# Two-layer hybrid trunk: the order of the first mixer, its startup and weight reuse, the place of an output product, and casts moved to ScalarE

## The chip, the cores and the metric

The kernel runs on one NeuronCore of a Trainium2 chip. The metric is device time in microseconds (us) of one execution, the median of three runs, of which one was recorded by the hardware profiler with the instructions, waits and transfers of every engine.

## The reference

The input is a sequence of 1024 tokens with 1024 features in float32, and one conditioning vector c. Two layers follow each other, each with a token mixer and an FFN. Every sub-layer is normalised and modulated (adaLN): six vectors per layer come out of a product of c with a large matrix, and give a scale, a shift and a gate.

```
    cond = jax.nn.silu(c)
    for i in range(DEPTH):
        mod = (cond @ ada_w[i] + ada_b[i])[:, None, :]
        sh1, sc1, g1, sh2, sc2, g2 = jnp.split(mod, N_MOD, axis=-1)
        ...
        h = rmsnorm(x, norm_mix_g[i]) * (1.0 + sc1) + sh1
        ...
        x = x + g1 * y
        h = rmsnorm(x, norm_ffn_g[i]) * (1.0 + sc2) + sh2
        x = x + g2 * (jnp.square(jax.nn.relu(h @ ffn_w1[i])) @ ffn_w2[i])
```

Here y is the output of the token mixer for h. The first mixer (RG-LRU, width 1280) is a product to two branches, a causal convolution of width 4 on one, a GELU on the other, two sigmoid gates out of 256 x 256 blocks, then the recurrence h[t] = a[t] h[t-1] + sqrt(1 - a[t]^2) (i[t] x[t]), a product with the gate branch and a product back to 1024. The second mixer (DSA) has 16 query heads of 64 on one shared key and value; an indexer of 8 heads scores all earlier tokens, the 256 best of a token take part in its softmax. The FFN is 1024 to 4096 to 1024 with squared ReLU.

## The kernel before, in words

Activations lie transposed, features on the 128 partitions and tokens along the row; the 1024 tokens go as two halves of 512 (h = 0 and 1). Every float32 product is made of three passes in a 32-bit reduced format, `mm3` (L337 to L339): a value is split into a high part (a cast, `wh`) and a low part (the remainder, `wl`), and high x high, low activation x high weight and high activation x low weight are added in PSUM. Weights pass through `weights()`: a block of 512 KB is loaded raw by SP's queue, ScalarE casts `wh` (L322), POOL subtracts for `wl` (L325). The first time a block is used, both parts are written to a DRAM copy (`part`, L330), and the second half reads these two parts back instead.

The program is written as Python generators and a few lists: what stands in the text order is the order on each engine. `pump` and `mix` put pieces of background lists (`fill`, `bg`) between the main steps. The adaLN work of later sub-layers is a series of `mac` steps in `fill` (a transfer of 256 KB on ScalarE's queue, then L433 or L435 on VectorE), ended by `fin` (transposes, L442).

**Startup** (`startup`, 0 to about 90 us) computes the scale and shift of the first norm for 8 blocks of 128 features: for each block VectorE sums eight 128 x 256 blocks of the matrix (`mac`, L519 and L521), TensorE transposes the sums (`cols`, L527), and VectorE reduces. Between them go the first six output blocks of the mixer's input product for the first half; then x's second half is loaded, squared and transposed (`turn_x`, L469), and its norm taken.

**The first mixer** (`mixer0`) has 5 groups (u) of 256 channels and runs a list `plan` of steps, each named by a letter, groups and the half: c (input product and convolution), g (GELU branch), l (gates and recurrence, `lru`), o (output product of the groups named). `lru` has two tiles, each with tanh, exp, tanh, square on ScalarE, and then two square roots (L652), which need another table of functions than the tanh and exp do; the table is loaded by an instruction of its own, ACT_TABLE_LOAD. In the end ScalarE casts the result (L663), POOL subtracts (L664), and output matmuls need both. The residual sum of the output products is L682. A norm is three parts: `stat` (squares summed by one-column matmuls, L71), `bc` (a broadcast to all partitions, L84), and `apply` (L98 to L104).

**FFN and layer 1.** `f1` is the first FFN product, with squared ReLU, `f2` the second, added to the residual by VectorE (L174). In layer 1, `kv_steps`, `qi_steps` and `q_group` make the keys, index queries and queries per token block and head group; `split_heads` makes the two parts of the queries (a VectorE cast L818, a POOL subtraction L819), and `turn4` transposes them (L827). `idx_steps` and `topk_steps` score the tokens and find the threshold. `attention(h)` goes through 16 units (token block, head group g, parity): scores (L1071, L1072), mask (L1083), exponential (L1089), reciprocal (L1092), POOL's normalising (L1094), transposes (L1099), product with the values (L1111, L1112). `proj_out(h, g1, g)` is the output product of head group g. In the last stage `store` transposes the result back (L1193) and writes it.

## Time and profile before

| | before |
|---|---|
| median of three runs | 2618.0 us (2617.76 to 2620.06) |
| profiled execution: time | 2617.35 us |
| profiled execution: span | 2615.6 us |
| TensorE busy | 2427.1 us (93%) |
| VectorE busy | 1546.9 us (59%) |
| ScalarE busy | 1231.0 us (47%) |
| POOL busy | 996.4 us (38%) |

The time of the profiled execution lies 1.75 us above its span. The busy time of TensorE contains matmuls at the lower of the clock's two levels; the mean granted clock over the span is 0.97. The profile's engine names are PE (TensorE), DVE (VectorE), ACT (ScalarE), POOL and SP.

### The profile page before, as it was taken

The numbers are of one execution on the slowest core, as the hardware profiler recorded it, in microseconds if no ns is written. First come the engines' busy times: TensorE is split into PE (matmuls) and PEld (weight loads), VectorE is DVE, ScalarE is ACT, GpSimd is POOL, SyncE is SP. The second block draws the span as 40 slices with busy tenths as digits, with TensorE's granted clock in tenths as the row PEclk, the third lists the DMA queues.
The fourth block names the chain that finished last, engine by engine and source line by source line (L and its number), as shares of the span: only waits on it lengthen the run. The fifth ranks groups of instructions, "written<-read, shape, count | busy, mean of one in ns | idle before, by whom it ended". The sixth has DMA issues, their size and how long they took to land. (4 is left out here: it accounts for less than half of the span.)

```text
span 2615.6 us, 30703 instructions
## 1 busy us (share of the span) xinstructions
PE 2427.1 (93%) x10834; PEld 1948.6 (74%) x10834; DVE 1546.9 (59%) x2873; ACT 1231.0 (47%) x2158; POOL 996.4 (38%) x584
## 2 busy tenths in 40 slices
PE   5689899898999999999996998999998998999999
PEld 3567678676788888888776876888887786788887
DVE  8677775579934421376686875575579894421212
ACT  3466463541122143235535767768753884433322
POOL 3454411222121244230136932223235996444342
PEclk7899999999999999999998998999999999999999
DMA  8677656326611278754431212223240003322231
GB/s 241 243 251 248 211 208 238 123 81 216 202 49 49 97 250 292 276 174 163 145 99 27 96 51 73 84 82 101 82 137 9 1 9 121 113 89 97 89 102 60
DMA packets 202748, 345.14 MB, mean 132 GB/s; under 512 B 19594, under 2 KB 109410, under 8 KB 202594
## 3 DMA queue, kind: packets, MB, share of 16 engines
q1 hardware_dynamic: 173648, 297.91, 33.6%
q10 hardware_dynamic: 28946, 45.27, 5.2%
q8 instruction: 85, 1.39, 0.2%
q14 instruction: 69, 0.57, 0.1%
HBM read 270.77 MB, written 72.35 MB: 131 GB/s over the span
## 5 line engine op out<-in xcount | busy, mean ns | idle before, releaser
L325 POOL TENSOR_TENSOR wl<-raw,wh 128x1024 fp32r<-128x1024 f32 (+2 forms) x242 | 597.1, 2476 | 1175.1 <-ACT wh L322 1128.2
L322 ACT CAST wh<-raw 128x1024 fp32r<-128x1024 f32 (+2 forms) x275 | 282.7, 1031 | 594.6 <-PE ps L338 270.7
L337 PE MATMUL ps<-a,wh 128*128 128x512 f32 x1152 | 462.5, 404 | 41.1 <-DVE a L682 13.9
L338 PE MATMUL ps<-a,wh 128*128 128x512 f32 x1152 | 461.4, 401 | 3.7 <-POOL a L664 2.2
L339 PE MATMUL ps<-a,wl 128*128 128x512 f32 x1152 | 459.4, 399 | 0.0
L337 PE MATMUL pd<-a,wh 128*128 128x512 f32 x1072 | 429.1, 401 | 21.6 <-DVE xc L595 13.8
L338 PE MATMUL pd<-a,wh 128*128 128x512 f32 x1072 | 428.0, 399 | 7.1 <-DVE a L100 5.7
L339 PE MATMUL pd<-a,wl 128*128 128x512 f32 x1072 | 427.2, 399 | 0.0
L174 DVE SCALAR_TENSOR_TENSOR a<-ps,mod,a 128x512 f32<-128x512 f32 x352 | 260.1, 745 | 264.2 <-PE ps L339 263.5
L337 PEld LDWEIGHTS ps<-a,wh 128*128 128x128 f32 x1152 | 220.0, 191 | 100.8 <-DVE a L682 16.0
L338 PEld LDWEIGHTS ps<-a,wh 128*128 128x128 f32 x1152 | 219.7, 191 | 57.9 <-POOL a L664 4.0
L339 PEld LDWEIGHTS ps<-a,wl 128*128 128x128 f32 x1152 | 219.2, 190 | 53.5
L337 PEld LDWEIGHTS pd<-a,wh 128*128 128x128 f32 x1072 | 202.4, 189 | 74.0 <-issue 14.5
L338 PEld LDWEIGHTS pd<-a,wh 128*128 128x128 f32 x1072 | 203.1, 189 | 59.8 <-DVE a L100 8.2
L339 PEld LDWEIGHTS pd<-a,wl 128*128 128x128 f32 x1072 | 203.1, 189 | 49.1
L1094 POOL TENSOR_SCALAR s<-s,rr 128x128 f32<-128x128 f32 (+7 forms) x128 | 224.9, 1789 | 22.3 <-DVE rr L1092 22.3
L337 PE MATMUL ps<-hid,wh 128*128 128x512 f32 x512 | 204.6, 400 | 12.9 <-DVE a L174 12.9
L978 ACT ACTIVATE signs<-sc,tc 128x384 int8<-128x384 f32 (+5 forms) x186 | 164.1, 882 | 92.9 <-DVE tc L993 79.4
L339 PE MATMUL ps<-hid,wl 128*128 128x512 f32 x512 | 204.0, 398 | 0.0
L338 PE MATMUL ps<-hid,wh 128*128 128x512 f32 x512 | 204.0, 398 | 0.0
L435 DVE SCALAR_TENSOR_TENSOR a<-a,cond,a 128x512 f32<-128x512 f32 x140 | 132.0, 974 | 45.0 <-DMA a<-in_ada_w_dram 44.3
L337 PEld LDWEIGHTS ps<-hid,wh 128*128 128x128 f32 x512 | 97.2, 190 | 39.4 <-DVE a L174 15.2
(270 smaller groups left out, 3715.9 us busy)
## 6 DMA issues: line engine op xcount, KB each, us to landing
raw<-in_ffn_w_dram SPq DMA_DIRECT2D x192, 512.0 KB, 3.6
a<-in_ada_w_dram ACTq DMA_DIRECT2D x160, 256.0 KB, 3.7
part<-wh SPq DMA_DIRECT2D x61, 512.0 KB, 3.6
part<-wl SPq DMA_DIRECT2D x61, 512.0 KB, 3.0
wh<-part SPq DMA_DIRECT2D x61, 512.0 KB, 3.3
wl<-part SPq DMA_DIRECT2D x61, 512.0 KB, 4.5
raw<-in_a_w_in_dram SPq DMA_DIRECT2D x20, 512.0 KB, 6.4
st<-in_ada_w_dram SPq DMA_DIRECT2D x32, 256.0 KB, 4.2
```

The costliest lines, as they stand in the source:

```text
L174: nc.vector.scalar_tensor_tensor(xt, ps, self.g2[:, m:m + 1], xt, op0=OP.mult, op1=OP.add)
L322: nc.scalar.copy(wh, raw)
L325: eng.tensor_tensor(wl, raw, wh.bitcast(FT), op=OP.subtract)
L337: pe.matmul(out, wh, xh, start=start, stop=False)
L338: pe.matmul(out, wh, xl, start=False, stop=False)
L339: pe.matmul(out, wl, xh, start=False, stop=stop)
L435: nc.vector.scalar_tensor_tensor(a, r, s, a, op0=OP.mult, op1=OP.add)
L978: A.activation(self.signs[:, 0:L], sc, AF.Sign, bias=0.0 if neg is None else neg.bitcast(FT), accum_out=n)
L1094: G.tensor_scalar(sl[e][:, 0:L], sl[e][:, 0:L], r[:, e:e + 1], None, op0=OP.mult)
```

## The change

The change has eight parts.

1. **Startup columns.** For the blocks 0 to 3 (NS = 4) the adaLN sums are made by TensorE: for scale and shift, eight one-column matmuls each (L559 of the changed kernel). For the blocks 4 to 7 only the scale is, and VectorE sums 128 x 128 for the shift. x's second half, its squares, transposes and norm sums become a step `second` at the head of the mixer's plan.
2. **The plan of the first mixer** is another list: each recurrence comes one step after its convolution with another projection or an output product between, the output products are "o010", "o20", "o340" and "o011", "o21", "o341", the adaLN `fin`, the norms and the FFN's first block take other places, and one `pump` follows each step.
3. **One square root** in `lru` covers both tiles (128 x 1024).
4. **Weights.** Mixer blocks keep only `wl` in DRAM; at the second use the raw block is loaded again, ScalarE casts it again, and `wl` is read back. FFN blocks are kept as before. Output weights of attention are now kept in this way too. The writes of the copies are issued two blocks later.
5. **adaLN loads** are issued one `mac` ahead.
6. **FFN of layer 0:** the first four steps of `f2` for half 0 come ahead of the first product of half 1.
7. **Layer 1's queries:** in query groups ScalarE does the first cast of `split_heads`. The transposes of group g = 1 go to a list of their own, which the attention takes up after its first unit. The indexer steps of blocks 6 and 7 (11 of 16) go between and after `stat` and `bc` of the FFN's norm, no longer into the FFN's background. Before the last attention, two steps of `f2` go between the two query groups.
8. **The output product** of head group 0 for the last attention runs in that attention's background from unit 12 on. `store` goes in pieces: the first half's between `stat` and `bc` of the last norm, a part of the second half's into the last FFN.

```
+            while (k, 0) not in st:
+                self.loads.pop(0)()
+            if self.loads:
+                self.loads.pop(0)()
...
         def cols(kt):
             ps = self.ps()
-            for e in range(2):
-                nc.tensor.transpose(ps[:, e * P:(e + 1) * P], sums[kt][:, e * P:(e + 1) * P], self.ident)
-            t = self.small([P, 2], "mt")
-            V.tensor_reduce(t, ps[:, 0:256].rearrange("p (e k) -> p e k", e=2), axis=AX.X, op=OP.add)
+            for e in range(2 if kt < NS else 1):
+                for k in range(KT):
+                    nc.tensor.matmul(ps[:, e:e + 1], view(kt, k, e), self.cond[:, k:k + 1],
+                                     start=k == 0, stop=k == KT - 1)
...
-            for m in range(2):
-                A.activation(v[m], v[m], AF.Sqrt, scale=0.25)
+            A.activation(vv, vv, AF.Sqrt, scale=0.25)
...
+        if kept:
+            nc.sync.dma_start(wl.bitcast(FT), kept[0])
+            return wh, wl
...
-            for w in (wh, wl):
+            for w in (wl,) if isinstance(key[0], str) else (wh, wl):
                 d = self.dram.tile([P] + shape, FT, name=self.nm("part"))
-                nc.sync.dma_start(d, w.bitcast(FT))
+                self.late.append((d, w.bitcast(FT)))
...
-            plan = ["g10", "l00", "l10", "c20", "g20", "o010", "l20",
-                    "c30", "g30", "l30", nB, "c40", "g40", "o230", "l40",
-                    "c01", "g01", "o40", "l01", "c11", "g11", "l11", "c21", "g21", "o011", "l21",
-                    lambda: N["f0", 0].stat(), "c31", "g31", "c41", "l31", "g41", "o231", "l41", nA,
-                    lambda: f1(0), "o41", f1b]
+            plan = [lambda: self.second(), "g10", "l00", "c20", "l10", "g20", "c30", fin, "o010", "l20", "g30", "c40",
+                    "l30", "g40", nB, "o20", "l40", "c01", "g01", "o340", "l01", "c11", stat0, "g11", "c21", "l11",
+                    "g21", "c31", "o011", "l21", "g31", "c41", "l31", "g41", nA, "o21", "l41", f1a, "o341", f1b]
...
-            nc.vector.tensor_copy(zv[:, :, 0:64], rv)
+            (nc.scalar.copy if parity else nc.vector.tensor_copy)(zv[:, :, 0:64], rv)
...
+            if k and self.late_turns:
+                late()
             self.pump()
...
+            some(4)
             N["f1", 0].stat()
+            some(4)
             N["f1", 0].bc()
             hf[0] = N["f1", 0].apply(mod[1, 4], mod[1, 3])
-            for t in (6, 7):
-                self.fill += self.idx_steps(t) + [lambda t=t: self.fill.extend(self.topk_steps(t))]
+            some(3)
+            self.fill += heads + self.topk_steps(6) + self.topk_steps(7)
...
+            def background():
+                yield from f2
+                while self.units < 12:
+                    yield
+                self.reload(1)
+                self.rate = 0.45
+                yield from self.proj_out(1, mod[1, 2], 0)
+
+            self.bg, self.rate = background(), 0.8
             self.banks(False)
             self.attention(1, before)
             self.finish()
-            self.reload(1)
-            run(self.proj_out(1, mod[1, 2], 0))
             run(self.proj_out(1, mod[1, 2], 1, sqs("f1")))
```

On TensorE, in the startup, before (`ma` is VectorE's sum, `pd` and `ps` are PSUM tiles):

```order
L469 MATMUL ps_178<-ident,st_97 128x128
L84 MATMUL ps_195<-nl_189,ones 128x512
L527 MATMUL ps_291<-ident,ma_282 128x128 x2
L527 MATMUL ps_329<-ident,ma_311 128x128 x2
L337 MATMUL pd_198<-a_301,wh_307 128x512
```

And now, at the same place (`cond` is c, `st` the loaded block of the matrix):

```order
L492 MATMUL ps_178<-ident,st_97 128x128
L84 MATMUL ps_195<-nl_189,ones 128x512
L559 MATMUL ps_284<-cond,st_204 128x1 x4
L559 MATMUL ps_284<-cond,st_207 128x1 x4
L559 MATMUL ps_323<-cond,st_214 128x1 x4
L559 MATMUL ps_323<-cond,st_217 128x1 x4
L351 MATMUL pd_200<-a_304,wh_310 128x512
```

The two transposes of each of VectorE's sums have become one-column matmuls straight on the loaded blocks (each of the rows shown for a block stands twice, for scale and shift), so that nothing on VectorE is between the load and TensorE's sums.

On TensorE, at the last recurrence of the first mixer, before (`ps_3882` is a gate product of that recurrence, L84 the broadcast of the norm behind it, `ps_4044` the output product that needs the recurrence):

```order
L338 MATMUL ps_3882<-a_3559,wh_3843 128x512
L339 MATMUL ps_3882<-a_3558,wl_3845 128x512
L84 MATMUL ps_3915<-nl_3324,ones 128x512
L337 MATMUL ps_4044<-a_3903,wh_4040 128x512
L338 MATMUL ps_4044<-a_3904,wh_4040 128x512
L339 MATMUL ps_4044<-a_3903,wl_4042 128x512
```

And now (`ps_3898` is the gate product, `pd_3942` the FFN's first block, `ps_4011` the output product):

```order
L352 MATMUL ps_3898<-a_3568,wh_3860 128x512
L353 MATMUL ps_3898<-a_3567,wl_3861 128x512
L353 MATMUL pd_3942<-a_3750,wl_3939 128x512
L351 MATMUL pd_3942<-a_3756,wh_3938 128x512
L352 MATMUL pd_3942<-a_3757,wh_3938 128x512
L353 MATMUL pd_3942<-a_3756,wl_3939 128x512
...
L351 MATMUL ps_4011<-a_3634,wh_4007 128x512
```

The FFN's first block stands between the last gate products and the output product (13 matmuls of it behind the gates), and the norm's broadcast has moved ahead of all of it.

On TensorE, at the beginning of the first attention, before (`a` of L1071 are keys, L827 are query transposes, L1099 the softmax's first transposes, L778 a key and value product):

```order
L1071 MATMUL ps_11055<-a_8195,a_10235 128x384
L1072 MATMUL ps_11055<-a_8197,a_10235 128x384
L827 MATMUL ps_11097<-identR,a_10782 128x128 x4
L827 MATMUL ps_11103<-identR,a_10785 128x128 x4
...
L827 MATMUL ps_11127<-identR,a_10813 128x128 x4
L1099 MATMUL ps_11133<-ident,s_10857 128x128 x4
L778 MATMUL ps_11142<-wh_10887,a_10609 128x328
```

And now (L1124, L874, L1152 and L825 to L827 are the same operations in the changed kernel):

```order
L1124 MATMUL ps_11084<-a_8224,a_10264 128x384
L1125 MATMUL ps_11084<-a_8226,a_10264 128x384
L1152 MATMUL ps_11126<-ident,s_10886 128x128 x4
L825 MATMUL ps_11135<-wh_10916,a_10638 128x328
L826 MATMUL ps_11135<-wl_10917,a_10638 128x328
...
L1152 MATMUL ps_11139<-ident,s_10969 128x128 x4
...
L874 MATMUL ps_11151<-identR,a_10811 128x128 x4
```

The six groups of query transposes that stood ahead of the softmax's first transposes are now behind them and spread over the key and value products.

## Rows read from the trace of the kernel before

**Rows 1.** Page: engine, busy us (share of the span), instructions.

```profile
PE 2427.1 (93%) x10834; PEld 1948.6 (74%) x10834; DVE 1546.9 (59%) x2873; ACT 1231.0 (47%) x2158; POOL 996.4 (38%) x584
```

**Rows 2.** Stages: length; busy PE, PEld, DVE, ACT, POOL (records); PEclk, DMA share, GB/s.

```profile
0.00:84.00 84.00, 48.78 (x189) 35.22 (x189) 66.34 (x148) 31.47 (x45) 33.37 (x25) 0.84 0.75 227
84.00:155.00 71.00, 50.10 (x205) 39.16 (x205) 44.72 (x57) 43.09 (x67) 30.56 (x16) 0.86 0.72 249
155.00:260.00 105.00, 98.13 (x408) 76.41 (x408) 81.89 (x93) 62.66 (x87) 55.72 (x25) 0.98 0.74 257
260.00:336.00 76.00, 56.93 (x222) 44.02 (x221) 56.66 (x73) 36.94 (x48) 31.62 (x15) 0.89 0.64 214
336.00:510.00 174.00, 170.78 (x740) 136.45 (x738) 107.18 (x154) 89.16 (x124) 28.99 (x20) 1.00 0.56 200
510.00:570.00 60.00, 50.48 (x201) 38.49 (x202) 47.59 (x64) 29.20 (x43) 14.02 (x7) 0.89 0.12 39
570.00:705.00 135.00, 120.56 (x511) 94.60 (x510) 120.26 (x162) 25.99 (x36) 29.09 (x11) 0.96 0.65 209
...
1330.00:1475.00 145.00, 119.75 (x632) 103.61 (x631) 108.50 (x297) 82.71 (x223) 94.66 (x95) 0.86 0.18 54
...
1540.00:1600.00 60.00, 47.78 (x206) 38.12 (x205) 47.89 (x93) 37.05 (x77) 9.02 (x6) 0.86 0.14 44
1600.00:1980.00 380.00, 380.00 (x1636) 306.09 (x1635) 232.50 (x524) 257.59 (x436) 110.46 (x48) 1.00 0.29 93
1980.00:2250.00 270.00, 243.94 (x1288) 196.47 (x1287) 204.25 (x416) 170.66 (x332) 211.12 (x125) 0.96 0.13 42
...
2600.00:2615.60 15.60, 9.91 (x59) 8.22 (x57) 4.83 (x7) 2.25 (x4) 0.00 (x0) 0.93 0.36 135
```

**Rows 3.** The instructions of line L521: min/median/max ns, first and last start.

```profile
L521 DVE SCALAR_TENSOR_TENSOR ma<-st,cond,ma x56: 470/478/2147, 17.0 to 73.0; 128x256 f32<-128x256 f32 x56
```

**Rows 4.** Timeline, startup and mixer: start, length, engine, instruction [idle before, releaser].

```profile
28.33 0.66 PE L527 MATMUL ps<-ident,ma 128*128 128x128 f32 x2 [9.91 <-DVE ma L521]
...
97.11 2.25 DVE L433 TENSOR_SCALAR a<-a,cond 128x512 f32<-128x512 f32 x1 [2.18 <-DMA a<-in_ada_w_dram]
...
103.86 0.77 PE L337 MATMUL pd<-a,wh 128*128 128x512 f32 x1 [11.44 <-DVE xc L595]
...
265.93 0.79 PE L337 MATMUL ps<-a,wh 128*128 128x512 f32 x1 [5.59 <-DVE ns L102]
...
332.82 0.79 PE L337 MATMUL ps<-a,wh 128*128 128x512 f32 x1 [7.67 <-DVE a L682]
...
509.49 0.63 ACT L652 ACTIVATE v<-v 128x512 f32<-128x512 f32 x1
510.14 1.28 ACT L645 ACT_TABLE_LOAD   x1
...
516.20 0.80 PE L337 MATMUL ps<-a,wh 128*128 128x512 f32 x1 [9.08 <-ACT a L663]
```

**Rows 5.** Timeline of TensorE, layer 1, columns as in rows 4.

```profile
1395.11 0.75 PE L827 MATMUL ps<-identR,a 128*128 128x128 f32 x4 [7.28 <-POOL a L819]
...
1575.08 1.87 PE L71 MATMUL ps<-ones,nl 128*128 128x1 f32 x8 [6.18 <-DVE nl L63]
1581.40 2.05 PE L84 MATMUL ps<-nl,ones 128*128 128x512 f32 x2 [4.45 <-DVE tl L991]
...
2178.47 0.47 PE L1099 MATMUL ps<-ident,s 128*128 128x128 f32 x1 [4.33 <-POOL s L1094]
...
2236.83 1.05 PE L71 MATMUL ps<-ones,nl 128*128 128x1 f32 x8 [2.69 <-DVE nl L63]
```

**Rows 6.** A stretch of the startup, columns as in rows 2.

```profile
19.00:40.00 21.00, 7.96 (x19) 5.38 (x20) 20.90 (x41) 6.42 (x10) 11.14 (x8) 0.51 1.03 276
```

**Rows 7.** Page: ScalarE's weight casts, xcount | busy, mean ns | idle before, releaser.

```profile
L322 ACT CAST wh<-raw 128x1024 fp32r<-128x1024 f32 (+2 forms) x275 | 282.7, 1031 | 594.6 <-PE ps L338 270.7
```

More of the change, by code (lines that the diff above doesn't have):

```diff
@@ L421, in ada, with load @@
         st = {}
+        def load(k):
+            for c in range(2):
+                st[k, c] = self.tile()
+                o = j * D + c * 512
+                nc.scalar.dma_start(st[k, c], self.i["ada_w"][l, k * P:(k + 1) * P, o:o + 512])
+        self.loads += [lambda k=k: load(k) for k in range(KT)]
         def mac(k):
@@ L927, in turn @@
                 self.turned.add((T, g, p))
[L929 removed]
+            turns.append([lambda p=p, turn=turn: turn(p) for p in range(2)])
             yield
@@ L1049, in attention, with late @@
         heads = [(u, i) for u in units for i in range(0, 4, step)]
+        def late():
+            for f in self.late_turns.pop(0):
+                f()
         def qk(u, i0):
@@ L1297, in run @@
             self.ada_fill([(1, 1, self.gmix(1)), (1, 0), (1, 2), (1, 4, self.gffn(1)), (1, 3), (1, 5)])
-            F.load2(0, 0), F.load2(0, 1)
+            F.load2(0, 0)
+            f2 = F.f2_steps([0], 0)
+            for _ in range(4):
+                next(f2)
             F.f1(0, 1), F.f1(1, 1)
+            F.load2(0, 1)
+            run(f2)
+            F.f2([0], 1)
             for p in range(NJ):
```

170 lines of the change are left out of this document (106 added, 64 removed).

## The prediction

> **What bounds the kernel now.** I read the page's table of engines first, then one table of engine busy time by stage, and then, in the stages with loss, the timeline rows of TensorE's waits. The table of engines [rows 1] shows TensorE busy for 93% of the span, so only work that TensorE does at the lower clock, its waits, or work taken off it can pay. The table by stage [rows 2] says where these are. In the saturated attention and FFN stretch of 1600 to 1980 TensorE has 380.00 us of work in 380.00 us at full clock, and one record takes 380/1636 = 0.232 us; nothing can be won there. The losses lie in the other rows: idle time is the stage's length less TensorE's busy time, and a stage with a mean granted clock c spent 2(1-c) of its length at the lower level (1.2 GHz). Idle are: 0 to 84: 35 us; 84 to 155: 21; 155 to 260: 7; 260 to 336: 19; 336 to 510: 3; 510 to 570: 10; 570 to 705: 14; 1330 to 1475: 25; 1540 to 1600: 12; 1980 to 2250: 26; 2600 to the end: 6. Together that is 178 us, plus what the lower clock costs behind each wait. The change rearranges the order in nearly all of these stages and hardly touches the saturated ones, so I go stage by stage, with the profiled execution (2617.35 us, 0.65 us under the median) as base.
>
> **Startup, 0 to 84.** Here the adaLN column sums run on VectorE: the instruction of L521 takes 0.478 us at the median, and TensorE waits 9.91 us for one at 28.33 [rows 3, 4]. VectorE is busy 66 of these 84 us [rows 2]. The change takes the row blocks 0 to 3 off it altogether (4 x 8 x 0.478 = 15.3 us) and halves the other four in width (between 0 and 7.6 us). In return TensorE gets 96 one-column matmuls in the program, which are 192 records. Their form is not in the startup before; the nearest rows are the eight one-column records of L71, once 1.05 us and once 1.87 us [rows 5], so 0.131 or 0.234 us each, and 25 or 45 us for all. TensorE's 144 wide records of the stage need 144 x 0.232 = 33 us; most of the other 45, transposes, lie before that wait. The wait at 28.33 begins at 28.33 - 9.91 = 18.4 us; columns and wide records from there on, without a wait, end at 18 + 25 + 33 = 76 against 84, a gain of 8, of which I take 4 since not every wait goes. But in 19 to 40 the granted clock is 0.51 [rows 6]. If it stays there while blocks 0 to 3 are summed, their 128 records cost 128 x 0.234 = 30 us and the 72 wide ones of these blocks 72 x 0.464 = 33; the other 64 one-column records (8) and the other 72 wide ones (17) follow: 18 + 30 + 33 + 8 + 17 = 106, 22 us late. The term is a gain of 4, its bounds a gain of 14 (the later waits of the stage shortened too) and a loss of 22.
>
> **84 to 155.** TensorE waits 11.44 us at 103.86 for the first convolution, VectorE having stood at 97.11 for an adaLN weight transfer with that convolution queued behind it [rows 4]. After the change these transfers are issued one step ahead, and the transposes of x's second half go behind the first convolutions. The gap and its lower clock cost about 11 + 6; the transposes and squares that have moved come back later (some 32 short records and four copies, about 5). I take 10 of the 21 idle us, between 3 and 18.
>
> **155 to 570, the mixer.** The plan now puts a projection between a convolution and its recurrence. In 155 to 260 only 7 us are idle, I take 4. In 260 to 336 two waits stand, 5.59 us at 265.93 and 7.67 at 332.82 [rows 4], 13.3 together, both behind one long VectorE series with nothing else for TensorE to do; the new order has an FFN norm and projections elsewhere, and I take 12 of the 19 us (bounds 4 and 22, with the clock). In 510 to 570 the wait of 9.08 us for the last recurrence's cast [rows 4] is what the order rows show filled by FFN matmuls; VectorE has 48 of 60 us there, so some wait remains, and I take 6 (bounds 0 and 15).
>
> The square root of both tiles in one instruction halves the table loads, from 41 in the program to 21. One lasts 1.28 us [rows 4], so ScalarE does 20 x 1.28 = 26 us less. It is off TensorE's path except at the last recurrence, where one load and one cast stand between the data and the wait; that is inside the 6. The Trainium skill ("ScalarE: Activation LUTs", section "What ACT_TABLE_LOAD costs") counts a drain of about 1.38 us beside each load, 2.66 us in all; by it the saving on ScalarE would be an estimated 53 us, and the last wait 1.4 us more to win. The rows here show no such drain, for the square root ends at 509.49 + 0.63 = 510.12 and the next load begins at 510.14 [rows 4].
>
> The price of this is in the weights: for the mixer's second use of a block only the low part is read back, and the high part is cast again on ScalarE. That is 29 more casts of 1.031 us [rows 7], 30 us, in 260 to 570. Between 336 and 510 ScalarE is busy 89 of 174 us [rows 2], so the casts fit beside TensorE's work; I count -2, with bounds of 0 and 30. In layer 1 eight casts and eight subtractions on POOL fall away in the last stage, off the path.
>
> **570 to 705.** VectorE is busy 120 of 135 us there [rows 2]: the FFN's second product is written back by it. The first four steps of the second product now come before the first product of the other half, so that its write-back begins earlier and is spread over more of TensorE's work. I take 5 of 14 us, with bounds 0 and 10.
>
> **Layer 1.** At 1395.11 TensorE waits 7.28 us for POOL's splitting of the query, ahead of the first attention work [rows 5], and the granted clock of the stage is 0.86, so some 41 us pass at the lower level. The order rows show these query transposes behind the first transposes of the softmax now, and half of the split's first casts go to ScalarE, which has 83 of 145 us [rows 2]. To be had are these 7.28 us and about 10 of clock, half of the 20 that 41 us at the lower level can cost; I take 9 (0 to 17). In 1540 to 1600 the norm's waits of 6.18 and 4.45 us [rows 5] get eleven indexer steps around them: I take 7 (0 to 14), since the clock is held too. In 1980 to 2250 the second part of the queries gets two FFN steps in between (3 of the idle us), and the output product of the first heads goes into the last attention's background. POOL is busy 211 of 270 us there and TensorE waits on its normalising, 4.33 us at 2178.47 [rows 5]. POOL's work does not shrink, so the attention itself cannot end much sooner: only TensorE's idle time in it can be filled, not all 26 us; I take 8 more (0 to 14). The last stage: stores of one half drawn forward, 2 of its 6 idle us.
>
> **The sum.** 4 + 10 + 4 + 12 - 2 + 6 + 5 + 9 + 7 + 3 + 8 + 2 = 68 us. From 2617 that is 2549, and against the median 2550.
>
> **Rivals.**
> A. *The startup stays at the lower clock.* For it: 0.51 in 19 to 40, in which TensorE has work for 8 of 21 us [rows 6], and single-column work is small. Against it: these columns give TensorE something to do in the very gap. The startup ends 22 late instead of 4 early: 2550 + 26 = 2576. The Trainium skill ("TensorE: Matmul & The Clock Gate", section "HAM oscillation — how this bites in real kernels") says that groups of matmuls with waits between them start cold each time; by that rule this rival happens, and the stretch at 0.51 agrees with it.
> B. *Layer 1's engines, not its order, are the limit.* POOL is full in the last attention and VectorE has 48 of 60 us in 1540 to 1600 [rows 2]. Then 9 + 7 + 8 fall away: 2574.
> C. *The repeated casts are late, and the kernel gets slower.* The place is the mixer's second half, 260 to 570. A cast there stands in ScalarE's order behind a table load (1.28), two exponentials or roots and their waits, so a weight may come 3.2 us late (1.28 and three instructions of about 0.6), and 29 x 3.2 = 93 us more: 2550 + 93 = 2643. It decides from 68/29 = 2.3 us for each on. Against it: three raw buffers, and ScalarE idle half the time [rows 2].
> D. *VectorE carries the mixer.* It is busy 45 of 71, 82 of 105, 57 of 76 and 48 of 60 us in the stages from 84 on [rows 2], and a new order leaves that work as it is. The waits only move, and 10 + 4 + 12 + 6 go: 2582.
>
> **How the numbers follow.** A measurement of this kernel tells about 0.2% (5 us) from no change. The forecast, 2530 to 2566 by the stage bounds, gets 0.62; A 0.13 (2576), B 0.10 (2574), D 0.09 (2582), C 0.06 (2643). All but C lie more than 0.2% below 2618; I leave 0.02 for several of A, B and D together ending within 0.2%, taken from them. So faster 0.92, same 0.02, slower 0.06. The range from 2520 to 2586 holds the forecast, A, B and D one at a time, and leaves out C, most mixtures and a part of the bounds on the gain's side.
>
> **What would show it.** Right: the one-column rows in the startup at 0.13 us and the last block's matmuls done before 80; no TensorE gap over 5 us behind a recurrence; TensorE's gaps at about 1395 and 1575 gone, and the stages' mean clock near 1. TensorE's busy time would fall only by the cold stretches. Wrong: casts of L328 as the releaser of TensorE's waits (C); the startup's clock at 0.5 past 50 us (A); VectorE as the releaser of gaps as long as now in the mixer (D); POOL still ahead of gaps over 4 us with the output product left behind (B).

## The result, and the profile after

The changed kernel takes 2588.93 us (median of four runs, 2585.56 to 2592.21), the kernel before in the same measurement 2617.88 us: the ratio is 0.9884, 95% interval 0.9872 to 0.9897. It is faster by 29 us. The forecast was 2550 us with a range of 2520 to 2586: the sign is right, the gain is less than half of the 68 us, and the time lies 3 us above the range. The profiled execution has a span of 2587.3 us.

TensorE's row of the page, which answers to [rows 1]:

```profile
PE 2449.9 (95%) x11014; PEld 1976.0 (76%) x11014; DVE 1500.7 (58%) x2802; ACT 1234.9 (48%) x2187; POOL 965.9 (37%) x575
```

TensorE is busy 23 us more in a span 28 us shorter, with 180 records more: its idle time has fallen, and a good part of the place has been filled with the new columns. Where it still waits is seen by stage; the stretches are cut at the same events as in the table below (columns as in [rows 2]), and the second and the fourth are shorter ones around two waits:

```profile
0.00:92.60 92.60, 77.62 (x369) 66.39 (x370) 42.91 (x106) 31.37 (x44) 33.22 (x26) 0.83 0.64 196
85.00:108.00 23.00, 7.91 (x37) 5.81 (x37) 13.92 (x17) 8.96 (x14) 11.12 (x5) 0.83 1.01 356
108.00:170.00 62.00, 60.87 (x261) 48.81 (x262) 43.70 (x53) 42.52 (x73) 31.66 (x16) 0.95 0.46 156
170.00:185.20 15.20, 1.09 (x6) 0.59 (x5) 12.08 (x16) 8.42 (x12) 7.32 (x4) 0.68 0.73 235
185.20:312.00 126.80, 116.25 (x481) 92.28 (x481) 106.75 (x125) 64.81 (x89) 59.12 (x27) 0.94 0.55 180
312.00:554.00 242.00, 230.33 (x966) 181.46 (x967) 155.95 (x222) 132.71 (x180) 48.64 (x31) 0.97 0.51 171
1343.00:1512.00 169.00, 149.01 (x844) 127.48 (x845) 132.63 (x355) 118.41 (x314) 124.98 (x131) 0.94 0.32 109
1991.00:2209.00 218.00, 204.84 (x1138) 165.22 (x1137) 164.01 (x337) 155.78 (x310) 175.50 (x103) 0.99 0.19 65
```

The times at which the same events stand in the two traces (us from the start of the span) tell where the 28 us come from:

| event | before | after | gained so far |
|---|---|---|---|
| first convolution of the mixer (ScalarE) | 92.53 | 92.62 | -0.1 |
| first convolution of the second half | 308.39 | 302.28 | 6.1 |
| last recurrence's cast of the mixer | 520.43 | 521.32 | -0.9 |
| first matmul of the FFN's second product | 557.95 | 553.95 | 4.0 |
| norm ahead of layer 1 (first half) | 1103.52 | 1095.17 | 8.4 |
| norm of the other half | 1353.40 | 1342.90 | 10.5 |
| first attention, last product with values | 1532.35 | 1512.42 | 19.9 |
| last attention, first scores | 2012.42 | 1991.18 | 21.2 |
| last norm's `stat` | 2236.83 | 2208.64 | 28.2 |
| end of the last engine instruction (a copy on VectorE) | 2611.89 | 2583.56 | 28.3 |

Startup and mixer together gave 4 us, where the forecast had 34 (4 + 10 + 4 + 12 - 2 + 6). Layer 0's FFN gave 4, the first attention 9, what lies between it and the last norm 8. Three rows of the table say less than they seem to. In the nine kernels of this document that share this startup, the changed one and eight of the experiments, the first convolution stands between 87.2 and 93.5 us, so a difference of 5 us there is no result. Ahead of the first convolution of the second half the old list has one group's output product more ("o230" for "o20"), so the 6.1 us are in part moved work. And two steps of the FFN's second product now stand ahead of the last attention's first scores and not behind them. The columns and TensorE's main waits, in the timeline of the kernel after (they answer to [rows 4, 5]):

```profile
18.80 10.95 PE L559 MATMUL ps<-cond,st 128*128 128x1 f32 x64
...
107.80 0.76 PE L351 MATMUL pd<-a,wh 128*128 128x512 f32 x1 [12.30 <-DVE xc L641]
...
185.12 1.94 PE L465 MATMUL ps<-ident,a 128*128 128x128 f32 x8 [14.11 <-DVE a L458]
...
268.87 0.79 PE L351 MATMUL ps<-a,wh 128*128 128x512 f32 x1 [8.33 <-DVE a L728]
...
485.07 0.80 PE L351 MATMUL pd<-a,wh 128*128 128x512 f32 x1 [4.53 <-ACT a L103]
...
520.77 0.79 PE L351 MATMUL ps<-a,wh 128*128 128x512 f32 x1 [2.91 <-ACT a L709]
...
1380.55 0.64 PE L825 MATMUL ps<-wh,a 128*128 128x328 f32 x1 [4.38 <-DVE mn L1136]
...
1567.24 0.67 PE L84 MATMUL ps<-nl,ones 128*128 128x512 f32 x1 [2.26 <-DVE nl L79]
...
2121.11 0.33 PE L1152 MATMUL ps<-ident,s 128*128 128x128 f32 x1 [2.06 <-POOL s L1147]
```

The wait at the startup's first columns (9.91 us at 28.33) is gone: 64 one-column records stand in its place. The wait for the last recurrence fell from 9.08 to 2.91 us, those around the layer-1 norm from 6.18 and 4.45 to under 2.5, and the query transposes' 7.28 us are gone too. But the wait for the first convolutions is as long as before (12.30 for 11.44 us), a wait of 14.11 us stands ahead of `fin` that was not there, and one of 8.33 us at 268.87 stands where 5.59 and 7.67 were. New too are a wait of 4.53 us at 485.07, for the apply of the FFN's norm (L103), and in the first attention, in place of the 7.28 us, one of 4.38 us for the mask (L1136).

VectorE's timeline around the first and the second of these waits shows two different things. First it waits for adaLN transfers, with the convolutions (L641) behind them:

```profile
98.31 0.49 DVE L456 TENSOR_SCALAR a<-a,cond 128x512 f32<-128x512 f32 x1 [2.46 <-DMA a<-in_ada_w_dram]
99.74 1.25 DVE L456 TENSOR_SCALAR a<-a,cond 128x512 f32<-128x512 f32 x1 [0.94 <-DMA a<-in_ada_w_dram]
100.91 3.51 DVE L458 SCALAR_TENSOR_TENSOR a<-a,cond,a 128x512 f32<-128x512 f32 x2
104.35 0.74 DVE L641 SCALAR_TENSOR_TENSOR xc<-pd,col,xc 128x509 f32<-128x509 f32 x1
...
163.84 0.75 DVE L458 SCALAR_TENSOR_TENSOR a<-a,cond,a 128x512 f32<-128x512 f32 x1 [1.85 <-DMA a<-in_ada_w_dram]
164.51 2.91 DVE L696 SCALAR_TENSOR_TENSOR tg<-tg,xc 128x512 f32<-128x512 f32 x1
167.34 2.88 DVE L458 SCALAR_TENSOR_TENSOR a<-a,cond,a 128x512 f32<-128x512 f32 x1
...
173.16 4.48 DVE L704 TENSOR_TENSOR_SCAN hs<-la,tg 128x512 f32<-128x512 f32 x2
```

From 85 to 108 the transfers are full (share 1.01, 356 GB/s): the writes of weight parts, x's second half, the mixer's weights and the adaLN blocks all come at once. Then the last columns' sums, for which `fin` waits on TensorE, stand on VectorE behind a recurrence, and many of VectorE's instructions last several times their usual length: 2.9 us where the same line has rows of 0.74. POOL's timeline in the same stretch:

```profile
164.14 5.54 POOL L334 TENSOR_TENSOR wl<-raw,wh 128x1024 fp32r<-128x1024 f32 x2 [2.73 <-ACT wh L328]
172.93 2.51 POOL L334 TENSOR_TENSOR wl<-raw,wh 128x1024 fp32r<-128x1024 f32 x1 [3.25 <-ACT wh L328]
```

VectorE's long instructions lie beside these subtractions. Over 100 to 320 us of this trace, VectorE's instructions by whether a POOL instruction overlaps them (worked out from their starts and ends in the trace; number, median ns):

```
line                       alone         beside POOL
L458  (SBUF, SBUF)         15, 744       19, 1442
L704  scan (SBUF, SBUF)     4, 1194       6, 3390
L695  (SBUF, SBUF)          5, 691        5, 1749
L104  (SBUF, SBUF)          6, 744        2, 2568
L641  (PSUM, SBUF)         19, 744       13, 748
L728  (PSUM, SBUF)         10, 743        6, 742
```

Instructions that read one operand from PSUM are as long as ever; those with both tiles in SBUF are stretched. The rows above show how: POOL's subtraction ends at 172.93 + 2.51 = 175.44 us, and the first of the two scans, which began at 173.16 beside it, lasts 3.36 us, to 176.52, so it ends 1.08 us behind the subtraction, about its own 1.19 us. So it is with each of the 28 instructions of six lines with two SBUF tiles (L104, L458, L695, L696, L702, L704) that last over 1.3 times their median alone in these 220 us: each begins while a POOL subtraction runs, and what it exceeds that median by is the time to the subtraction's end, less 0.11 to 0.20 us. The Trainium skill ("SBUF — State Buffer", section "Who interferes with whom") states that a VectorE instruction with two SBUF inputs contends with a GpSimd instruction that reads SBUF, because its second input comes through a read interface that the two share, and that contention for the shared ports is an exclusive lock. The rows here agree (GpSimd is POOL). The forecast had VectorE's load from the stages of before, and nothing of this in its price of a new order.

### The profile page after: what moved, and what is told of

Same layout as the page of the kernel before. It is cut to its first block, busy times and chain, and to the rows that moved or that the text cites. A ratio compares the mean times of both kernels' runs of the same rounds, so it can differ in the third digit from the quotient of the medians.

```text
span 2587.3 us, 31024 instructions
## 1 busy us (share of the span) xinstructions
PE 2449.9 (95%) x11014; PEld 1976.0 (76%) x11014; DVE 1500.7 (58%) x2802; ACT 1234.9 (48%) x2187; POOL 965.9 (37%) x575
## 5 line engine op out<-in xcount | busy, mean ns | idle before, releaser
L334 POOL TENSOR_TENSOR wl<-raw,wh 128x1024 fp32r<-128x1024 f32 (+2 forms) x233 | 569.3, 2451 | 1102.3 <-ACT wh L328 1075.0
L328 ACT CAST wh<-raw 128x1024 fp32r<-128x1024 f32 (+2 forms) x296 | 305.5, 1035 | 599.9 <-PE ps L352 237.9
L351 PE MATMUL ps<-a,wh 128*128 128x512 f32 x1152 | 463.2, 405 | 20.3 <-DVE a L728 10.8
L351 PE MATMUL pd<-a,wh 128*128 128x512 f32 x1072 | 430.4, 402 | 18.8 <-DVE xc L641 14.2
L351 PEld LDWEIGHTS ps<-a,wh 128*128 128x128 f32 x1152 | 219.4, 191 | 76.7 <-DVE a L728 11.4
L351 PEld LDWEIGHTS pd<-a,wh 128*128 128x128 f32 x1072 | 203.8, 190 | 69.9 <-issue 15.9
L351 PE MATMUL ps<-hid,wh 128*128 128x512 f32 x512 | 205.0, 400 | 9.3 <-DVE a L174 6.5
L458 DVE SCALAR_TENSOR_TENSOR a<-a,cond,a 128x512 f32<-128x512 f32 x140 | 134.7, 994 | 34.5 <-DMA a<-in_ada_w_dram 34.3
L152 DVE TENSOR_TENSOR a<-r,a 128x512 fp32r<-128x512 f32 x64 | 47.1, 757 | 140.2 <-ACT a L151 138.9
```

What stands on the lines that cost most here:

```text
L152: nc.any.tensor_tensor(ql, r, qh.bitcast(FT), op=OP.subtract)
L328: nc.scalar.copy(wh, raw)
L334: eng.tensor_tensor(wl, raw, wh.bitcast(FT), op=OP.subtract)
L351: pe.matmul(out, wh, xh, start=start, stop=False)
L458: nc.vector.scalar_tensor_tensor(a, r, s, a, op0=OP.mult, op1=OP.add)
```

## The experiments

Theory after the result: the mixer's new order brings a gain, but it is lost to two things that it does not touch, the rush of transfers behind the startup and VectorE's work stretched beside POOL, and to TensorE's columns in the startup. Rivals: the order itself brings nothing (VectorE's load as such); ScalarE's repeated casts are late; the new place of `fin` is at fault. In each experiment the time of the changed kernel is 2589 us (ratio 0.9884); all ratios are to the kernel before, measured together with the kernel of the experiment, and a difference to the changed kernel is the difference of the ratios times 2618.

**adaLN sums earlier (fin).** The first edit stands behind each step of the plan, the second ahead of it.

```
-            self.pump()
+            self.pump(2 if k < 3 else 1)
...
-            self.pump(2)
+            self.pump(4)
```

> The changed kernel with four adaLN steps issued ahead of the first mixer's plan and two behind each of its first three steps, as in the kernel before (the changed one: two ahead, one behind each step). Theory (the place of fin holds TensorE): the 14.1 us wait at 185 falls under 4 us, and the time falls by 8 to 14 us, to 2575 to 2581 us. Rival (VectorE carries the first half of the mixer, so that steps drawn forward push its other work back): the wait at 185 gets shorter but waits of the same sum appear behind the first convolutions and recurrences; time within 3 us of 2589.

Measured: 2590.9 us, ratio 0.9893 (0.9878 to 0.9908): no change. The rival holds. In the timeline the wait for `fin` is gone; L351 at 187.19 below is the output product behind it. In its place the wait for the first convolutions is 17.10 us, for 12.30, and another of 6.42 us is new:

```profile
110.25 0.76 PE L351 MATMUL pd<-a,wh 128*128 128x512 f32 x1 [17.10 <-DVE xc L641]
...
166.05 0.77 PE L351 MATMUL pd<-a,wh 128*128 128x512 f32 x1 [6.42 <-DVE xc L641]
...
187.19 0.47 PE L351 MATMUL ps<-a,wh 128*128 128x512 f32 x1 [3.39 <-DVE adat L466]
```

So it is not the place of `fin`: whatever is put ahead of the other on VectorE, the other is late.

**The startup's sums on VectorE again.**

```
-            if kt < NS:
-                return
...
+                nc.tensor.transpose(ps[:, e * P:(e + 1) * P], sums[kt][:, e * P:(e + 1) * P], self.ident)
...
+            V.tensor_reduce(t, ps[:, 0:256].rearrange("p (e k) -> p e k", e=2), axis=AX.X, op=OP.add)
```

> The changed kernel with the startup's adaLN sums back on VectorE (128 x 256 blocks and two transposes each), everything else as changed. Theory (TensorE is now the bound of the startup; its last columns come at 84.7 instead of 75.9 us): first convolution about 9 us earlier, time 2578 to 2583 us. Rival (the startup is bound by something that both share, the order behind it takes the difference up): first convolution earlier, but the wait ahead of the second convolution longer by the same, time within 3 us of 2589. Forecast's own view (columns on TensorE gain 4): 2593.

Measured: 2584.56 us, ratio 0.9867 (0.9853 to 0.9882), 4.5 us less than the changed kernel, with intervals that overlap. The first convolution stands at 87.03 us and the mixer ends 11 us earlier in this profile, of which 3.4 are left at the end. The first convolution's place shows nothing by itself, since it stands at 87.21 us in one kernel with the columns too. The time goes the way of the theory, with about half its size, and is not clear of the intervals.

**Both weight parts kept.**

```
-            for w in (wl,) if isinstance(key[0], str) else (wh, wl):
+            for w in (wh, wl):
```

> The changed kernel with both weight parts of the mixer and of the attention's output product kept in DRAM and read back, so 29 casts of about 1.03 us fewer on ScalarE and as many 512 KB writes more. Theory (casts are hidden): time within 3 us of 2589, with 280 to 520 us of the same length. Rival (casts late on ScalarE cost TensorE): 5 to 15 us faster, the stretch from 300 to 520 shorter.

Measured: 2591.08 us, ratio 0.9889 (0.9870 to 0.9909): no change. The repeated casts cost nothing that can be measured; rival C of the forecast falls.

**Two square roots.**

```
-            A.activation(vv, vv, AF.Sqrt, scale=0.25)
+            for m in range(2):
+                A.activation(v[m], v[m], AF.Sqrt, scale=0.25)
```

> The changed kernel with the square root in two instructions again, tile by tile (still behind both tiles' other functions). Theory (table loads are off TensorE's path): within 3 us of 2589. Rival (ScalarE's table loads pace the recurrences): 5 to 20 us slower, up to 20 more table loads in the trace.

Measured: 2592.64 us, ratio 0.9895 (0.9874 to 0.9916), 3 us more and inside the intervals. This trace has 19 loads at the roots, where the changed kernel has 10, and 9 more at the tanh behind them, 39 in all for 21:

```profile
L699 ACT ACT_TABLE_LOAD  x19: 1283/1283/1283, 128.3 to 515.3; - x19
```

A table load costs ScalarE its 1.28 us, and TensorE next to nothing. ScalarE is idle for no more than 0.02 us ahead of any of these 28 loads and behind it.

**The last attention's output product behind it.**

```
-                while self.units < 12:
-                    yield
-                self.reload(1)
-                self.rate = 0.45
-                yield from self.proj_out(1, mod[1, 2], 0)
...
+            self.reload(1)
+            run(self.proj_out(1, mod[1, 2], 0))
```

> The changed kernel with the last attention's output product of head group 0 behind the attention again, not in its background. Theory (the product fills TensorE's waits on POOL and gives nearly all of layer 1's later gain): 5 to 9 us slower than the changed kernel's 2589, that is 2594 to 2598 us; the attention itself ends earlier, the product comes back as a stretch of about 22 us. Rival (POOL's pace sets the end of the attention and the product costs there what it saves behind): within 3 us of 2589.

Measured: 2592.08 us, ratio 0.9894 (0.9880 to 0.9907), 2.6 us more and inside the intervals. In the profile the attention ends 15.8 us earlier without the product in it (2164.87 for 2180.69), and the last norm stands 3.9 us later. The product does not lie in free time: most of it lengthens the attention. The rival holds.

**Indexer steps in the FFN's background.**

```
-            some(4)
             N["f1", 0].stat()
-            some(4)
             N["f1", 0].bc()
...
+            for t in (6, 7):
+                self.fill += self.idx_steps(t) + [lambda t=t: self.fill.extend(self.topk_steps(t))]
```

> The changed kernel with all indexer steps of blocks 6 and 7 in the FFN's background again, none around the norm. Theory (the steps fill the norm's waits of 6.2 and 4.5 us, but then the norm waits for VectorE's share of them, so that little is left): 1 to 4 us slower, 2590 to 2593. Rival (the forecast's 7 us hold and are lost elsewhere): 6 to 9 us slower, 2595 to 2598. Second rival (they cost): 2 to 5 us faster.

Measured: 2593.98 us, ratio 0.9899 (0.9885 to 0.9912), 4 us more, with intervals that overlap. The norm's waits are back, as in [rows 5]:

```profile
1557.80 1.86 PE L71 MATMUL ps<-ones,nl 128*128 128x1 f32 x8 [6.07 <-DVE nl L63]
...
1564.11 2.05 PE L84 MATMUL ps<-nl,ones 128*128 128x512 f32 x2 [4.45 <-DVE tl L1038]
```

These 10.5 us of waits, for 4.75 in the changed kernel (2.49 and 2.26), are worth some 4 us of time, a little over half of the forecast's 7.

**Query transposes in the common list.**

```
-            q1 = self.q_group(0, 1, hm[0], self.late_turns)
+            q1 = self.q_group(0, 1, hm[0], turns)
...
-            run(self.q_group(1, 1, hm[2], self.late_turns))
+            run(self.q_group(1, 1, hm[2], turns))
```

> The changed kernel with the query transposes of head group 1 in the common list again (before the first softmax transposes in the first attention), everything else as changed. Theory (this is the whole of the gain in the first attention, the 7.3 us wait at 1395 and the clock behind it): the wait is back at 5 to 8 us, time 2596 to 2601. Rival (the casts on ScalarE and the saved POOL work do it): within 3 us of 2589.

Measured: 2594.25 us, ratio 0.9909 (0.9895 to 0.9923), 6.5 us more, the intervals just touching. The wait is back in the row that answers to 1395.11 of [rows 5]:

```profile
1379.30 0.75 PE L874 MATMUL ps<-identR,a 128*128 128x128 f32 x4 [7.12 <-POOL a L866]
```

The first attention takes 178.4 us in this trace, 169.5 in the changed kernel's and 179.0 before; in the twelve other kernels that have the step it takes 172.6 to 175.1. So this step is the gain there, but the changed kernel's trace shows more of it (9) than the others do (3 to 6); the 6.5 us of time lie between.

**The mixer's old list of steps.** The list is the one of the kernel before, with the new step for the second half at its head, `fin` among the adaLN steps, and the number of adaLN steps per plan step as before.

```
-            plan = [lambda: self.second(), "g10", "l00", "c20", "l10", "g20", "c30", fin, "o010", "l20", ...
+            plan = [lambda: self.second(), "g10", "l00", "l10", "c20", "g20", "o010", "l20", ...
```

> The changed kernel with the mixer's list of steps, the adaLN steps' places and fin as in the kernel before; only the new step for the second half's transposes stays at its head. Startup columns, one square root, weights and loads as changed. Theory (the new list moves TensorE's waits and removes hardly any, since VectorE is the limit of the mixer's first half; fin's wait of 14 us takes back what it wins): within 4 us of 2589. Rival (the list brings the forecast's 20 to 32 us and the startup eats them): 15 us slower or more, 2604 us and above.

Measured: 2599.68 us, ratio 0.9921 (0.9908 to 0.9935): 9.7 us more than the changed kernel. Neither statement holds: the list is worth some 10 us, less than half of the 22 that the forecast gave it (4 + 12 + 6), and not nothing. Its stretch from the first convolution to the FFN's second product is 469.3 us here and 461.3 in the changed kernel.

**Four adaLN transfers in the startup.**

```
+            macs, fin = self.ada(0, 2)
             hm[0], first = self.startup(...)
...
-            macs, fin = self.ada(0, 2)
...
+            if kt >= 4:
+                self.loads.pop(0)()
```

> The changed kernel with the first four adaLN transfers of the mixer (2 x 256 KB each) issued in the startup, behind the steps of its blocks 4 to 7, in place of behind it. Theory (the wait of 12.3 us for the first convolutions at 107.8 is one for transfers: 16 queues are full from 85 to 108 and VectorE stands ahead of the convolution for an adaLN transfer): that wait falls under 6 us, 4 to 8 us faster, 2581 to 2585. Rival (VectorE itself is late): the wait stays within 2 us and the time within 3 us of 2589.

Measured: 2578.95 us, ratio 0.9844 (0.9831 to 0.9857): 10.5 us less. The theory holds, with more than it claimed. The transfers are as full as before from 87 to 110 (first row, a stretch), but the four adaLN blocks have landed by then (the last landing that the trace gives is at 84.2 us): the wait for the first convolutions is 1.38 us, and the wait ahead of `fin` is gone with it; what is left at 171, ahead of the output product, is half as long:

```profile
87.00:110.00 23.00, 16.85 (x64) 12.19 (x63) 17.63 (x26) 10.35 (x19) 13.77 (x7) 0.84 1.00 357
...
96.16 0.77 PE L351 MATMUL pd<-a,wh 128*128 128x512 f32 x1 [1.38 <-DVE xc L643]
...
171.15 1.22 PE L351 MATMUL ps<-a,wh 128*128 128x512 f32 x2 [6.72 <-ACT a L711]
```

**Both.** The edits of the startup's sums and of the early transfers together.

> The changed kernel with the startup's sums back on VectorE (as x2) and the first four adaLN transfers issued in the startup (as x9). Theory (two separate costs: the columns take up on TensorE what they free, and the transfers' rush behind the startup): the gains add, 4 to 8 us faster than x9's 2579, that is 2571 to 2575. Rival (both move the same end of the startup: x2 and x9 reach the first convolution at 87.0 and 87.1 us): within 3 us of 2579. Second rival (VectorE's sums now collide with the early transfers): slower than 2582.

Measured: 2576.14 us, ratio 0.9838 (0.9824 to 0.9852). That is within the intervals of the early transfers alone (0.9844), 1.6 us less: the first rival holds, and the two gains do not add up as the theory had it.

**Subtractions on VectorE in the mixer's first half** (with the early transfers; `lo` chooses the engine of the weights' subtraction).

```
             def nB():
+                self.lo = [1]
...
+            self.lo = [0]
             plan = [lambda: self.second(), "g10", "l00", "c20", ...
```

> x9 with the weights' subtractions of the mixer's first half on VectorE, not POOL (some 35 of 2.4 us on POOL, 1.2 to 1.4 us on VectorE). In the trace VectorE's scans last 1.19 us with POOL idle and 3.36 us beside a POOL subtraction, and other instructions between two SBUF tiles 0.74 and up to 2.9, those that read PSUM 0.74 either way. Theory (this stretching is what makes VectorE the limit of the first half): scans at 1.2 us in 87 to 284, the first half 5 to 10 us shorter, time 2569 to 2575. Rival (VectorE's added 43 us weigh as much as the stretching): within 4 us of 2579, scans at 1.2 us all the same. Second rival (VectorE is then late with everything): slower than 2585.

Measured: 2565.28 us, ratio 0.9794 (0.9781 to 0.9808): 13 us less than the early transfers alone, more than the theory's 4 to 10. Of the weights' subtractions 22 have moved, not 35, the last at 201 us. The rows of the scan lines (min, median and max ns) of the changed kernel, of the early transfers alone, and of this kernel; the first half is the form without `hlast`:

```profile
L704 DVE TENSOR_TENSOR_SCAN hs<-la,tg x10: 1193/3354/3425, 143.9 to 306.4; 128x512 f32<-128x512 f32 x10
```

```profile
L706 DVE TENSOR_TENSOR_SCAN hs<-la,tg x10: 1192/2284/3434, 135.7 to 292.9; 128x512 f32<-128x512 f32 x10
```

```profile
L706 DVE TENSOR_TENSOR_SCAN hs<-la,tg x10: 1192/1206/1218, 130.0 to 279.4; 128x512 f32<-128x512 f32 x10
```

No scan of the first half is stretched any more, and the first half (first convolution to the first one of the second half) is 189 us long, for 197 without this edit and 210 in the changed kernel, though VectorE has taken over POOL's subtractions. The rows of this half in the kernel before, the changed one, with early transfers, and with the subtractions moved as well:

```profile
92.50:308.40 215.90, 178.26 (x715) 138.69 (x716) 162.09 (x190) 127.26 (x177) 103.34 (x48) 0.92 0.68 237
92.60:302.30 209.70, 172.85 (x728) 137.91 (x727) 163.86 (x195) 117.32 (x179) 97.79 (x48) 0.91 0.57 189
87.10:284.40 197.30, 169.84 (x712) 133.22 (x712) 153.81 (x191) 118.47 (x180) 100.82 (x48) 0.95 0.59 201
83.60:272.40 188.80, 171.07 (x730) 135.15 (x729) 157.89 (x217) 118.82 (x180) 51.32 (x28) 0.95 0.65 221
```

TensorE's idle time in them is 37.6, 36.9, 27.5 and 17.7 us: the change itself took none of it away, and each of the two edits some 10 us. VectorE's busy time did not fall with the subtractions (153.8 to 157.9 us); what fell is the time by which its instructions exceed the shortest of their kind, from 39 to 17 us. That POOL's own results were late, and are not so any more, is no rival: of TensorE's 27.5 idle us with early transfers, POOL ended 0.5.

**The same without the early transfers.**

> The changed kernel with the weights' subtractions of the mixer's first half on VectorE, adaLN transfers as changed (not drawn forward). Theory (two causes of their own: POOL's subtractions stretch VectorE's work, the transfers' rush holds it): 6 to 12 us faster than the changed kernel, 2577 to 2583, with the wait ahead of the second convolution (12.3 us at 107.8) still there at 8 us or more. Rival (the subtractions help only where transfers are early): within 4 us of 2589. Second rival (the subtractions were the whole cause): within 3 us of x12's 2565.

Measured: 2583.24 us, ratio 0.9862 (0.9846 to 0.9877), 5.8 us less than the changed kernel, the intervals just touching, and at the lower edge of the theory's bounds. The wait for the first convolutions is still there:

```profile
106.20 0.77 PE L351 MATMUL pd<-a,wh 128*128 128x512 f32 x1 [9.12 <-DVE xc L641]
```

The stretching counts without the early transfers too, by these figures for less than half as much (5.8 for 13 us) as when the transfers are out of its way.

**The kernel before, with the subtractions on VectorE.** The two lines of the last edit, and nothing of the change.

> The kernel before, with nothing changed but the weights' subtractions of the mixer's first half on VectorE. Theory (POOL beside VectorE paces the first half in the old order of steps too, so an order alone could not bring the forecast's gain): 5 to 14 us faster than before, 2604 to 2613. Rival (in the old order TensorE waits for the recurrence's chain and not for VectorE's load): within 4 us of 2618.

Measured: 2616.99 us, ratio 0.9993 (0.9981 to 1.0004): no change. The theory falls for this kernel. The time lies within the rival's bounds, but the trace does not show the rival's reason: of the 33.7 us for which TensorE is idle in the first half, the convolutions (L595) end 13.2, the residual sums (L682) 8.4 and a recurrence's cast (L663) none, so that it waits mostly for VectorE here too. The edit also did less than in the changed kernel. 18 subtractions have moved, and the scans are as long as before, because the five long ones stand beside POOL's subtraction of the first tile's result (L664), which has not moved (rows of before and of this kernel):

```profile
L658 DVE TENSOR_TENSOR_SCAN hs<-la,tg x10: 1224/1712/2205, 134.9 to 308.4; 128x512 f32<-128x512 f32 x10
```

```profile
L658 DVE TENSOR_TENSOR_SCAN hs<-la,tg x10: 1224/1712/2208, 130.1 to 303.0; 128x512 f32<-128x512 f32 x10
```

The time by which VectorE's instructions exceed the shortest of their kind falls from 38 to 25 us, and VectorE is busy 165 us of this half, for 162 before. Whether the old order of steps or another of the change's parts makes the difference to the edit before stays open.

**All three** (early transfers, subtractions and the startup's sums on VectorE).

> x12 with the startup's sums on VectorE too, as in x10. Theory (with transfers early and subtractions on VectorE the columns on TensorE cost or save next to nothing, as x10 against x9): within 4 us of x12's 2565. Rival (columns on TensorE cost, now that the mixer behind them is not the limit): 5 to 8 us faster, 2557 to 2560.

Measured: 2560.12 us, ratio 0.9772 (0.9759 to 0.9785), 5.8 us less than with the columns on TensorE, the intervals just touching. The theory said within 4 us, the rival 5 to 8: the rival holds. This is the fastest version, 60 us under the kernel before and 29 under the changed one. TensorE's row of its page:

```profile
PE 2425.1 (95%) x10834; PEld 1950.4 (76%) x10834; DVE 1516.5 (59%) x2858; ACT 1234.5 (48%) x2189; POOL 914.1 (36%) x553
```

TensorE has 25 us of work less than in the changed kernel, and VectorE 16 more.

## Why the prediction was wrong

**The startup's term (a gain of 4) had the wrong sign**, and the step that failed is the sum 18 + 25 + 33 = 76. The wait was removed, as forecast, and the 192 records of the columns took 26.0 us from start to start, close to the forecast's 25 (0.11 us each at the upper level of the clock, 0.21 at the lower; 10.95 us for the first 64). It is the 33 us of the 144 wide records, priced at 0.232 us, that did not hold: they took 44 us (0.23 us each at the upper level, 0.43 at the lower), with 5 us of waits among them, and the last of them ended at 94.6 us, not at 76 (before at 88.2). The granted clock is the reason, in these stretches of the changed kernel (columns as in [rows 2]):

```profile
21.80:38.80 17.00, 17.00 (x64) 15.36 (x64) 9.02 (x30) 4.70 (x6) 5.55 (x5) 0.50 0.77 222
18.80:94.60 75.80, 70.87 (x343) 60.34 (x342) 38.73 (x87) 23.31 (x31) 31.69 (x19) 0.80 0.60 185
```

The clock fell to the lower level among the first columns and came back only at the end of the first block's wide products, though TensorE had no break in between. Filling the gap with columns did not keep the clock up. TensorE is now busy 77.6 of 92.6 us where it had been idle 35 of 84, and its busy time rose by 23 us, where the forecast's sign of being right was that it falls. Undoing the columns gained 4.5, 1.6 and 5.8 us in three settings; none of the three is clear of its intervals, and all point the same way. Rival A named the cause, the clock, and overrated its size (a loss of 22).

**The term for 84 to 155 (10) failed.** "These transfers are issued one step ahead" was right, and too little: the blocks are asked for inside the rush and land late. Four blocks in the startup gave the 10.5 us that the forecast had, in the place it named.

**The mixer's terms (4 + 12 - 2 + 6) failed at the step "the new order has ... projections elsewhere".** The order fills the old waits, and the old list costs 9.7 us; the wait for the last recurrence fell from 9.08 to 2.91 us as forecast, and 4.53 us of that came back at the FFN's norm ahead of it, which every kernel with the new list shows (3.1 to 4.6 us) and no kernel with the old one. In the first half, new waits for VectorE stand in place of the old ones (36.9 us idle, for 37.6): the adaLN sums late by transfers hold `fin` (14.11 us), and VectorE's instructions are two to three times as long beside POOL. Removing both gave 10.5 + 13 us. Rival D ("the waits only move") described the outcome and came nearest with 2582, but had only a part of its cause: transfers and the stretching beside POOL are not told from load in VectorE's busy time of [rows 2]. That the same move of subtractions gained nothing in the kernel before is not explained.

**Casts and table loads were right:** -2 for 29 more casts (measured no change), and the table loads off the path. Of the 2.66 us that the Trainium skill ("ScalarE: Activation LUTs", section "What ACT_TABLE_LOAD costs") counts for a load with its drain and the row's 1.28 us, the row stands in this case: 1.283 us for each of the 19, and no more than 0.02 us of idle time on either side. 18 loads more took 3 us, inside the interval.

**FFN of layer 0:** 4.4 us for 5, in one pair of profiles; no run takes this step back. **First attention:** 6.5 us for 9 by the time of the experiment, by the step named. **Norm:** about 4 for 7, inside overlapping intervals. **The two FFN steps between the queries** (3): no run shows them by themselves. **Output product in the attention:** 2.6 for 8, the term that was mis-sized in layer 1. "Only TensorE's idle time in it can be filled" was right, but the product made the attention 15.8 us longer; rival B held here in part. **The last stage:** 0 for 2 (375.1 us from the last norm to the end before, 374.9 after).

Added up: 34 became 4 in the startup and mixer, and the other 34 became 24, of which 2 stand in layer 1's first part, where the forecast had no term. Mending the transfers, the subtractions and the columns brings 2560 us, inside the forecast's own range, but with the columns taken back and two edits that the forecast did not have; it does not show that the terms were of the right size. The waits were there to be won, and what stood behind them on VectorE was not in the sum.

## What to carry to other kernels

Ask, for a wait that a new order is to fill, what the releaser itself will wait for in its new place: here VectorE stood behind transfers that all come right after the startup, and issuing them some steps earlier was worth as much as the whole new list. Work moved onto the engine that sets the time is paid at its record's length at the clock it will run at, and so is the work that stands behind it in the same stretch: here the columns cost what was forecast, and the products behind them a third more. Where an engine's instruction lasts several times the median of its line, look at what another engine does in that moment before counting its busy time as load. And where a move gains nothing, look whether it did what it was meant to do: in the kernel before, the stretched scans stood beside a subtraction that had not moved.

## What the runs showed of the hardware

VectorE's instructions with two SBUF tiles are stretched when they begin beside a POOL subtraction, a scan from 1.19 to 3.39 us: each of 28 ended about its own length behind that subtraction. Those with a PSUM operand are not (0.74 us either way).

A busy TensorE can stay at the lower level: in the changed kernel it was busy 17.00 of 17.00 us from 21.8 to 38.8 with a granted clock of 0.50, with one-column records first and wide ones behind them.

The same work takes some us more or less with the clock. The first attention of thirteen kernels that have the same code there took from 169.5 us (the changed kernel, 20.5 us of it at the lower level, 20 us idle) to 175.1 us (the old list, 37.5 us at the lower level, 20 us idle). Gains in the mixer of single profiles were partly given back there, without any other wait: a single profile's stage is good to some 5 us, and the ratios over several runs decide.
